# Mixer outputs read back early, HGRN2 keys scaled on VectorE, decay products beside the transposes

## The chip, the cores and the metric

The kernel runs on one core of one Trainium2 chip. The metric is device time in microseconds (us); lower is better. Engines are named as the profile names them: PE is TensorE (matmuls; PEld its weight loads), DVE is VectorE, ACT is ScalarE, POOL is GpSimd, SP is SyncE. A row whose engine ends in q (SPq, ACTq) is that engine issuing a transfer.

## The reference, cut to what matters

One layer is computed for a prompt of 1024 tokens and for 8 samples of 4 tokens each, so 1056 columns in all (`T`), in fp32:

```python
h = _rmsnorm(x, g_attn)
z = h @ w_in      # one projection, 6152 columns: q/k/v/a/b/out-gate of branch A, q/f/i/out-gate of branch B, two gates
# branch A (gated DeltaNet): causal conv of width 4 on q/k/v, SiLU, then the chunked gated delta rule
# branch B (HGRN2): f = lb + (1-lb)*sigmoid(fb); attention with decay exp(cumsum(log f)), in chunks
y_a = (_head_rmsnorm(o_a) * silu(oga)) @ w_branch_a
y_b = (_head_rmsnorm(o_b) * silu(ogb)) @ w_branch_b
mix = jax.nn.sigmoid(gate_a) * y_a + jax.nn.sigmoid(gate_b) * y_b
x = x + mix @ w_out
h2 = _rmsnorm(x, g_ffn)
gc, new_ffn = _causal_conv(h2 @ w_ffn_gate, ffn_buf, w_ffn_conv)      # width 3
x = x + (jax.nn.silu(gc) * (h2 @ w_ffn_up)) @ w_ffn_down
```

Model width 1024, four heads of 128 in each branch, FFN width 2816. The new states and convolution caches are outputs too.

## The kernel before, in words

**Products.** Every large product is made of three matmuls on two halves of each operand. `split` casts fp32 to `hi` (ACT, L83) and subtracts to get `lo` (DVE, L84); `mm3` then adds hi·hi (L109), hi·lo (L110) and lo·hi (L111). A weight is loaded by `load_w` (SP, L96, tile `wraw`) and split into `whi` and `wlo`. The activations of the first projection are `hhi` and `hlo`; the same two memory slots later hold `ohi` and `olo`, the split outputs of the two branches.

**Stages.** The start loads and normalises x. Then come the two mixers: four groups of 256 tokens of HGRN2 (`hgrn_group`, about 160 to 460 us of the profiled execution), and four of gated DeltaNet (`gdn_group`, about 460 to 790 us). Mixers are chains of small steps on PE, DVE, ACT and POOL. To fill PE's time in between, the columns of the first projection are computed by and by: `fill` holds a queue of projections, and each mixer generator hands back a number at its `yield`, which says how many steps of 24 matmuls (352 columns wide, so 24 × 0.16 us) `drive` records there. What remains of the queue is computed after the last group (`fill.drain()`). Then follow the branch projections and the merge, `w_out`, and the FFN, which are matmul after matmul.

**Order.** The kernel is written in Tile: a scheduler decides the order of each engine's instructions from priorities in order of the code and from its own estimate of readiness. Each engine and each queue runs its rows strictly in that order. A tile whose pool slot was used before waits until the earlier tile's last reader is done; by default a pool that takes over memory of a closed pool waits for all of that pool.

**One HGRN2 group** (`hgrn_attn`) has seven levels. A level is: matmuls of `kk` with `qf` on PE (L997, or L984 for the last two levels), a masked copy of their result into `ad` (DVE, L1004), then `qf` times the running decay (DVE, L1010) and `kk` times the running decay (POOL, L1011). The next level's matmuls need both. `conv_proj` (the width-4 convolution of branch A's q, k, v, and the FFN's convolution) runs among them: its tile `z` gets a zero pad and the cached rows from POOL (L212, L213), the projected columns from ACT (L218), and three of its taps are DVE operations (L231, tile `co`).

**One gated DeltaNet group** transposes q, k, v on PE (L689), copies them, then for each chunk and head builds a decay matrix `EE` (DVE L709 makes `A`, PE L710 multiplies it, ACT L711 takes the exponential, and DVE masks it), and uses it on the k·q product (PE L718, DVE L719 into `UA`). A triangular inverse follows on DVE, through memory and back (`dU`, `dX`), and its first matmul is L773.

**From mixers to branch projections.** Each group's outputs `og` go to HBM (`oT_d`; ACT's queue, L874). After the mixers' pool is closed, `raw` is loaded back from `oT_d` by three transfers on SP's queue (2112, 1536 and 576 KB, L1172), behind a load of the sample rows `x1s` (L1165), and is split into `ohi` and `olo`, 16 casts and 16 subtractions. The last two of the three transfers are written with two fill steps ahead of each. In the branch projection `sga` and `sgb` are the gates, loaded from `sg_d` (L1195).

Of the kernel before, what the change touches and what calls it, by code (L numbers as in the profile page):

```python
# [8 lines left out]
F32 = mybir.dt.float32  # L9
# [33 lines left out]
def hybrid_step(ctx: ExitStack, tc: tile.TileContext, ins, outs):  # L43
# [28 lines left out]
    nc.gpsimd.memset(pexp[:, 1, :], 0.5)  # L72

# [131 lines left out]
    def conv_proj(W, j, width, wT, cacheT, out_cache, dst, dst_s, zp, src=None):  # L205

        pad = width - 1
        per = pad + STEP
        zw = pad + SEQ + NBAT * per
        z = zp.tile([P, zw], F32, name="z", tag="z")  # L210
        zs = z[:, pad + SEQ:].rearrange("p (b t) -> p b t", t=per)
        nc.gpsimd.memset(z[:, 0:pad], 0.0)  # L212
        nc.gpsimd.tensor_copy(zs[:, :, 0:pad], cacheT.rearrange("p (b t) -> p b t", t=pad))  # L213

        def ev(nb, ps):
            a = nb * BW
# [42 lines left out]
    def qkv_work(W, j, kind, h, zp=None):  # L259
# [3 lines left out]
                             qkv_s[:, kind, h, :], zp or mp)  # L263
# [9 lines left out]
    def load_x(t):  # L273
        xts[t] = n1.tile([P, D], F32, name="xt", bufs=6)
        nc.sync.dma_start(out=xts[t][:rows(t)], in_=x_rows(t))
# [198 lines left out]
    def decay_beta():  # L474
        nc.scalar.activation(beta, ab[:, :, 4:8], AF.Sigmoid)
        uy = mp.tile([P, 4, NT, H], F32, name="uy", tag="z")
# [39 lines left out]
    qf_s = mp.tile([P, 2, H, 32], F32, name="qf_s", bufs=1)  # L516
    og_s = mp.tile([P, 2, H, 32], F32, name="og_s", bufs=1)

    junk = mp.tile([P, P], BF16, name="junk", bufs=1)

    def os_tile(shape, name):
        return mp.tile(shape, F32, name=name, tag="os", bufs=4)
# [84 lines left out]
    def sample_products(src, cols, nk):  # L607
# [7 lines left out]
        ps = [PSM() for _ in range(nk)]  # L615
# [52 lines left out]
    def gdn_group(g, St):  # L668
# [16 lines left out]
        sst = mp.tile([P, 2, 8], F32, name="sst")  # L685
        for p in range(8):
            ps = PSM()
# [4 lines left out]
            nc.scalar.activation(junk, ps[:, 2 * P:3 * P], AF.Square, accum_out=sst[:, 1, p:p + 1])  # L692
            yield 0.1
# [8 lines left out]
        nc.vector.tensor_tensor(pr, pr, beta[:, c0:c0 + 2, :].rearrange("p c h -> p (c h)"), ALU.mult)  # L702
        for p0 in range(0, 8, 4):
            EE = os_tile([P, 4, P], "EE")
            ps = PSM()
            for p in range(p0, p0 + 4):
                cc, h = pairs[p]
                A = mp.tile([P, P], F32, name="A")
                nc.vector.tensor_scalar(A, slow, gcol[:, c0 + cc, h:h + 1], None, op0=ALU.mult)  # L709
                nc.tensor.matmul(ps[:, (p - p0) * P:(p - p0 + 1) * P], A, tri, start=True, stop=True)  # L710
            nc.scalar.activation(EE.rearrange("p c i -> p (c i)"), ps, AF.Exp)  # L711
            nc.vector.tensor_tensor(EE, EE, eem[:, 1:2, :].broadcast_to([P, 4, P]), ALU.mult)
# [8 lines left out]
            yield 0.5  # L721
# [105 lines left out]
        o_sb = os_tile([P, 8, P], "o_sb")  # L827
# [43 lines left out]
        og = mp.tile([P, H, GW], F32, name="og", tag="z")  # L871
# [84 lines left out]
    def hgrn_attn(q, f, kk, tots, nch, nlev, attn, ad):  # L956
# [15 lines left out]
        for l in range(nlev):  # L972
# [38 lines left out]
            nc.gpsimd.tensor_tensor(kv[:, :, 0, :], kv[:, :, 0, :], tv[:, :, 1:2].broadcast_to(shp), ALU.mult)  # L1011
# [4 lines left out]
            yield 0.75  # L1016
        return tot

    def hgrn_group(g, St, attn, ad):
# [18 lines left out]
        o_sb = os_tile([P, 8, P], "o_sb")  # L1038
# [23 lines left out]
        og = mp.tile([P, H, GW], F32, name="og", tag="z")  # L1062
# [93 lines left out]
    store_conv_cache(cout, 12, 27, cq_p[0, 0], cq_s.rearrange("l b t c -> (l b t) c"), mp, "z")  # L1156
# [16 lines left out]
    fill.drain()  # L1173
    ohi = hslot(0, [P, 2 * H, T], F32R, "ohi")
# [214 lines left out]
```

## Time and profile before

| | |
|---|---|
| time, median of 3 runs | 1808.07 us (1807.83 to 1810.8) |
| the profiled execution | 1809.22 us, its span 1807.5 us |
| PE busy | 1730.7 us, 96% of the span |
| PEld busy | 1637.3 us, 91% |
| DVE busy | 877.2 us, 49% |
| ACT busy | 529.1 us, 29% |
| POOL busy | 183.0 us, 10% |
| moved by DMA | 159.52 MB, 88 GB/s over the span |

The profiled execution is 1.7 us longer than its span, and stands 1.15 us above the median, inside the runs. PE is the engine that is nearly always busy; the others work beside it. So the time is PE's busy time and its idle time, and each idle stretch of PE has a row that names what ended it.

### The profile page before, as it was taken

Reading aid. Unit: us, or ns where it says so; the run is one execution under the profiler, and the core shown is the slowest. Engines: PE = TensorE matmul, PEld = TensorE weight load, DVE = VectorE, ACT = ScalarE, POOL = GpSimd, SP = SyncE. Lnnn points to the kernel's source line nnn. Section 1 sums busy time; section 2 is a strip of 40 time slices with the busy share of each in tenths; the row PEclk is TensorE's granted clock in tenths of the full one; section 3 lists DMA queues with packets and bytes.
Section 4 is the critical chain, followed back from the end, with each engine's and each line's share of the span. In section 5 each row is a group of like instructions: output and inputs, shape, how many; then the busy total and the mean of one; then the engine's idle time right before and its main releaser. Section 6 shows DMA issues by size and latency. Waiting matters only on the chain.

```text
span 1807.5 us, 31280 instructions
## 1 busy us (share of the span) xinstructions
PE 1730.7 (96%) x13277; PEld 1637.3 (91%) x13277; DVE 877.2 (49%) x1478; ACT 529.1 (29%) x1158; POOL 183.0 (10%) x323
## 2 busy tenths in 40 slices
PE   7999899989999989987999999999999999999997
PEld 7999899889889988987999999989989899899896
DVE  5411545785535364435542734453453453554457
ACT  5443323433433343332110522112112112122122
POOL 2200213341101020100000100000000000000001
PEclk9999999999999899998999999999999999999999
DMA  7333234345254243236432211111111111111103
GB/s 210 96 101 110 90 111 141 118 129 159 75 161 116 92 141 106 61 104 200 138 104 87 59 48 36 52 40 41 44 47 47 47 47 47 47 48 47 47 27 109
DMA packets 200648, 159.52 MB, mean 88 GB/s; under 512 B 18638, under 2 KB 185184, under 8 KB 200489
## 3 DMA queue, kind: packets, MB, share of 16 engines
q1 hardware_dynamic: 171286, 119.14, 22.3%
q10 hardware_dynamic: 29222, 38.39, 6.2%
q8 instruction: 104, 1.70, 0.4%
q14 instruction: 36, 0.29, 0.1%
HBM read 117.74 MB, written 39.69 MB: 87 GB/s over the span
## 4 chain that ended last, share of the span: by engine, by line
PE 55%; DVE 4%; DMA 2%; ACT 1%; issue 1%; POOL 1%; SPq 0%; ACTq 0%; DVEq 0%; POOLq 0%
PE pd L109 17%; PE pd L110 17%; PE pd L111 17%; PE pd L121 1%; DVE y L1348 1%; DMA raw<-oT_d 1%; DVE Pt L752 0%; DVE tmp L177 0%; PE pd L120 0%; ACT tmp L174 0%; DVE X L754 0%; POOL rs L76 0%; DVE mlo L84 0%; PE pd L123 0%; DMA Yd<-dX 0%
## 5 line engine op out<-in xcount | busy, mean ns | idle before, releaser
L109 PE MATMUL pd<-hhi,whi 128*128 128x352 f32 x1056 | 350.7, 332 | 0.0
L111 PE MATMUL pd<-hhi,wlo 128*128 128x352 f32 x1056 | 345.7, 327 | 0.0
L110 PE MATMUL pd<-hlo,whi 128*128 128x352 f32 x1056 | 344.6, 326 | 0.0
L109 PE MATMUL pd<-mhi,whi 128*128 128x352 f32 x1056 | 340.5, 323 | 0.0
L110 PE MATMUL pd<-mlo,whi 128*128 128x352 f32 x1056 | 338.6, 321 | 0.6 <-DVE mlo L84 0.6
L111 PE MATMUL pd<-mhi,wlo 128*128 128x352 f32 x1056 | 338.3, 321 | 0.0
L84 DVE TENSOR_TENSOR wlo<-wraw,whi 128x1024 fp32r<-128x1024 f32 x126 | 155.4, 1242 | 213.4 <-ACT whi L83 213.0
L83 ACT CAST whi<-wraw 128x1024 fp32r<-128x1024 f32 x126 | 130.4, 1049 | 399.4 <-PE pd L111 202.0
L109 PEld LDWEIGHTS pd<-hhi,whi 128*128 128x128 f32 x1056 | 200.3, 190 | 2.0 <-issue 0.6
L110 PEld LDWEIGHTS pd<-hlo,whi 128*128 128x128 f32 x1056 | 200.6, 190 | 0.8
L111 PEld LDWEIGHTS pd<-hhi,wlo 128*128 128x128 f32 x1056 | 200.4, 190 | 0.8
L110 PEld LDWEIGHTS pd<-mlo,whi 128*128 128x128 f32 x1056 | 198.4, 188 | 1.3 <-DVE mlo L84 0.9
L109 PEld LDWEIGHTS pd<-mhi,whi 128*128 128x128 f32 x1056 | 198.0, 188 | 0.4
L111 PEld LDWEIGHTS pd<-mhi,wlo 128*128 128x128 f32 x1056 | 198.0, 188 | 0.0
L1315 DVE TENSOR_TENSOR x<-x,pd 128x512 f32<-128x512 f32 x176 | 119.0, 686 | 78.0 <-PE pd L111 77.7
L109 PE MATMUL pd<-whi,act 128*128 128x512 f32 x352 | 138.1, 392 | 0.1
L110 PE MATMUL pd<-wlo,act 128*128 128x512 f32 x352 | 137.2, 390 | 0.0
L111 PE MATMUL pd<-whi,act 128*128 128x512 f32 x352 | 137.0, 389 | 0.0
L218 ACT COPY z<-pd 128x352 f32<-128x352 f32 (+1 forms) x102 | 44.1, 442 | 141.6 <-PE pd L111 138.3
L1292 DVE TENSOR_TENSOR ga<-pd,ga 128x352 f32<-128x352 f32 x66 | 34.5, 523 | 98.5 <-PE pd L111 98.5
L109 PEld LDWEIGHTS pd<-whi,act 128*128 128x128 f32 x352 | 66.1, 188 | 16.2 <-PE pd L111 1.6
L109 PE MATMUL pd<-ohi,whi 128*128 128x352 f32 x192 | 62.8, 328 | 18.3 <-ACT ohi L83 18.3
(418 smaller groups left out, 2622.8 us busy)
## 6 DMA issues: line engine op xcount, KB each, us to landing
wraw<-in_w_in SPq DMA_DIRECT2D x48, 512.0 KB, 4.5
wraw<-in_w_ffn_gate SPq DMA_DIRECT2D x22, 512.0 KB, 4.4
wraw<-in_w_ffn_up SPq DMA_DIRECT2D x22, 512.0 KB, 3.8
wraw<-in_w_ffn_down SPq DMA_DIRECT2D x22, 512.0 KB, 4.4
sg_d<-sg ACTq DMA_DIRECT2D x16, 528.0 KB
qkv_d<-sl ACTq DMA_DIRECT2D x12, 512.0 KB, 3.6
sga<-sg_d SPq DMA_DIRECT2D x12, 352.0 KB, 7.0
sgb<-sg_d SPq DMA_DIRECT2D x12, 352.0 KB, 2.9
```

Of the source, the lines that this page charges most:

```text
L83: nc.scalar.copy(out=hi, in_=src)
L84: (eng or nc.vector).tensor_tensor(lo, src, hi.bitcast(F32), ALU.subtract)
L109: nc.tensor.matmul(ps, whi[:, kw], xhi[:, kx], start=q == 0, stop=False)
L110: nc.tensor.matmul(ps, whi[:, kw], xlo[:, kx], start=False, stop=False)
L111: nc.tensor.matmul(ps, wlo[:, kw], xhi[:, kx], start=False, stop=q == n - 1)
L121: nc.tensor.matmul(ps[:NS], st[:, kx, 0:NS], wlo[:, kw], start=False, stop=False)
L218: nc.scalar.copy(out=z[:, pad + a:pad + e], in_=ps[:, :e - a])
L1292: nc.vector.tensor_tensor(a[:, bs], ps, a[:, bs], ALU.mult)
L1315: nc.vector.tensor_tensor(x1[:, t, qs], x1[:, t, qs], ps, ALU.add)
L1348: nc.vector.scalar_tensor_tensor(yt[:n, qs], x1t(t)[:n, qs], rs[:n], last["g"][:n, qs], ALU.mult, ALU.mult)
```

## The change

Five things are changed, in the code's order.

1. `conv_proj`: the zero pad and the cached rows of `z` are copied by ACT (from a constant tile `zero`), no longer by POOL.
2. Pools: the mixers' tiles `z`, `uy`, `og` and three small ones move into a pool of their own (`mz`); `o_sb` gets a tile of its own, and the tag `os` has three buffers in place of four; `xt` has five in place of six. The sample products of each branch go into one PSUM bank, cleared by one matmul with `zero`, in place of one or two banks.
3. `gdn_group`: the decay matrices `EE` (the operations of L709 to L712) are made inside the loop of the transposes; the yields around them are 0.2 (new) and 0.4 (was 0.5).
4. `hgrn_attn`: `kk` is scaled on DVE, no longer on POOL; the yield of a level is 0.7 (was 0.75).
5. The boundary: the pool `post` waits tile by tile (`reuse_waits="tile"`), `raw` is its first tile, and the load of `x1s` comes behind the loads of `raw`.

```diff
+    zero = const.tile([P, P], F32, name="zero")
+    nc.gpsimd.memset(zero, 0.0)
+
...
-        nc.gpsimd.memset(z[:, 0:pad], 0.0)
-        nc.gpsimd.tensor_copy(zs[:, :, 0:pad], cacheT.rearrange("p (b t) -> p b t", t=pad))
+        nc.scalar.copy(out=z[:, 0:pad], in_=zero[:, 0:pad])
+        nc.scalar.copy(out=zs[:, :, 0:pad], in_=cacheT.rearrange("p (b t) -> p b t", t=pad))
...
     def os_tile(shape, name):
-        return mp.tile(shape, F32, name=name, tag="os", bufs=4)
+        return mp.tile(shape, F32, name=name, tag="os", bufs=3)
...
-        ps = [PSM() for _ in range(nk)]
+        ps = PSM()
+        nc.tensor.matmul(ps[:, :nk * P], zero, cols.rearrange("p a h t -> p (a h t)"), start=True, stop=False,
+                         skip_group_check=True)
...
-                    nc.tensor.matmul(ps[a][32 * h:32 * h + 32, 0:P], zc[:, a * H + h, 32 * b:32 * b + 32],
-                                     Sb[:, h, :], start=b == 0, stop=b == NBAT - 1, skip_group_check=True)
...
+        EEs = []
         for p in range(8):
+            cc, h = pairs[p]
             ps = PSM()
             for q, kind in enumerate((0, 2, 1)):
                 nc.tensor.transpose(out=ps[:, q * P:(q + 1) * P], in_=col(kind, p), identity=ident)
             nc.vector.tensor_copy(kvt[:, p].rearrange("p a d -> p (a d)"), ps[:, 0:2 * P])
             nc.scalar.activation(junk, ps[:, 0:P], AF.Square, accum_out=sst[:, 0, p:p + 1])
             nc.scalar.activation(junk, ps[:, 2 * P:3 * P], AF.Square, accum_out=sst[:, 1, p:p + 1])
+            if p % 4 == 0:
+                pe = PSM()
+            A = mp.tile([P, P], F32, name="A")
+            nc.vector.tensor_scalar(A, slow, gcol[:, c0 + cc, h:h + 1], None, op0=ALU.mult)
+            nc.tensor.matmul(pe[:, (p % 4) * P:(p % 4 + 1) * P], A, tri, start=True, stop=True)
+            if p % 4 == 3:
+                EE = os_tile([P, 4, P], "EE")
+                nc.scalar.activation(EE.rearrange("p c i -> p (c i)"), pe, AF.Exp)
+                nc.vector.tensor_tensor(EE, EE, eem[:, 1:2, :].broadcast_to([P, 4, P]), ALU.mult)
+                EEs.append(EE)
             yield 0.1
         pr = mp.tile([P, 8], F32, name="pr")
...
+        yield 0.2
         for p0 in range(0, 8, 4):
-            EE = os_tile([P, 4, P], "EE")
-            ps = PSM()
-            for p in range(p0, p0 + 4):
-                cc, h = pairs[p]
-                A = mp.tile([P, P], F32, name="A")
-                nc.vector.tensor_scalar(A, slow, gcol[:, c0 + cc, h:h + 1], None, op0=ALU.mult)
-                nc.tensor.matmul(ps[:, (p - p0) * P:(p - p0 + 1) * P], A, tri, start=True, stop=True)
-            nc.scalar.activation(EE.rearrange("p c i -> p (c i)"), ps, AF.Exp)
-            nc.vector.tensor_tensor(EE, EE, eem[:, 1:2, :].broadcast_to([P, 4, P]), ALU.mult)
+            EE = EEs[p0 // 4]
             nc.vector.tensor_tensor(kgs[:, p0:p0 + 4], EE[:, :, P - 1], pr[:, p0:p0 + 4], ALU.mult)
             for p in range(p0, p0 + 4):
...
-            yield 0.5
+            yield 0.4
...
-        o_sb = os_tile([P, 8, P], "o_sb")
+        o_sb = mp.tile([P, 8, P], F32, name="o_sb", bufs=1)
...
             nc.vector.tensor_tensor(qv[:, :, 1, :], qv[:, :, 1, :], tv[:, :, 0:1].broadcast_to(shp), ALU.mult)
-            nc.gpsimd.tensor_tensor(kv[:, :, 0, :], kv[:, :, 0, :], tv[:, :, 1:2].broadcast_to(shp), ALU.mult)
...
-            yield 0.75
+            yield 0.7
         return tot
...
-    store_conv_cache(cout, 12, 27, cq_p[0, 0], cq_s.rearrange("l b t c -> (l b t) c"), mp, "z")
+    store_conv_cache(cout, 12, 27, cq_p[0, 0], cq_s.rearrange("l b t c -> (l b t) c"), mz, "z")
     for gen in side:
         drive(gen)
...
-    post = ctx.enter_context(tc.tile_pool(name="post", bufs=1))
+    post = ctx.enter_context(tc.tile_pool(name="post", bufs=1, reuse_waits="tile"))
+    raw = post.tile([P, 2 * H, T], F32, name="raw", tag="m1")
     mhi = post.tile([P, KD, T], F32R, name="mhi", tag="m0")
     x1s = post.tile([32, D], F32, name="x1s")
-    nc.sync.dma_start(out=x1s, in_=x_rows(NC))
-    raw = post.tile([P, 2 * H, T], F32, name="raw", tag="m1")
     last = (NG - 1) * GW
     for x, a, b in ((1, 0, T), (0, 0, last), (0, last, T)):
         if a:
@@ -1171,6 +1181,7 @@
             fill.step()
         nc.sync.dma_start(out=raw[:, x * H:(x + 1) * H, a:b], in_=oT_d[x][:, :, a:b].rearrange("h p t -> p h t"))
     fill.drain()
+    nc.sync.dma_start(out=x1s, in_=x_rows(NC))
     ohi = hslot(0, [P, 2 * H, T], F32R, "ohi")
```

**SP's queue at the boundary** (names: `raw` is the read-back, `wraw` the next weights of the branch projection, `sga` and `sgb` the gates, `res` rows of x for `w_out`). Before:

```order
L1195 DMA sga<-sg_d_92 128x2x352
L96 DMA wraw<-in_w_branch_a 128x4x128
L96 DMA wraw<-in_w_branch_b 128x4x128
L1165 DMA x1s<-in_x_sample 32x1024
L1172 DMA raw<-oT_d_91 128x4x1056
L1172 DMA raw<-oT_d_90 128x4x768
L1172 DMA raw<-oT_d_90 128x4x288
L1195 DMA sgb<-sg_d_93 128x2x352
```

With the change:

```order
L1206 DMA sga<-sg_d_94 128x2x352
L1182 DMA raw<-oT_d_93 128x4x1056
L1182 DMA raw<-oT_d_92 128x4x768
L1182 DMA raw<-oT_d_92 128x4x288
L1184 DMA x1s<-in_x_sample 32x1024
L1206 DMA sgb<-sg_d_95 128x2x352
L1206 DMA sga<-sg_d_94 128x2x352
L1239 DMA res<-in_x_prompt 128x2x256 x3
L99 DMA wraw<-in_w_branch_a 128x4x128
L99 DMA wraw<-in_w_branch_b 128x4x128
```

The three loads of `raw` have moved ahead of a pair of weight loads and of `x1s`, directly behind the first `sga`.

**ACT at the same place** (`sg` is the last gate that the fill computes; `whi` a cast of branch weights). Before:

```order
L564 ACTIVATE sg<-pd 128x352
L83 CAST whi<-wraw 128x8x128
L565 DMA sg_d_93<-sg 128x1056
L83 CAST ohi<-raw 128x352 x4
L83 CAST ohi<-raw 128x2x352 x4
L83 CAST ohi<-raw 128x352 x4
L83 CAST ohi<-raw 128x2x352 x4
```

With the change:

```order
L568 ACTIVATE sg<-pd 128x352
L86 CAST ohi<-raw 128x352
L569 DMA sg_d_95<-sg 128x1056
L86 CAST ohi<-raw 128x352 x7
L86 CAST ohi<-raw 128x2x352 x8
L86 CAST whi<-wraw 128x8x128 x2
```

The first four and the next four rows of before are branch B's part of `raw`; branch A's, with which the first product begins, came after them. Now the eight narrow casts, of both branches' first 352 columns, stand first, and two weight casts stand behind all sixteen.

**DVE in the second HGRN2 group** (`ad` is the masked copy of a level's result, `qf` and `kk` the scaled operands, `co` the convolution, `wlo` a weight's low half). Before:

```order
L1004 COPY_PREDICATED ad<-lmask_u,pm 128x64x2
L1010 TENSOR_TENSOR qf<-qf,tots 128x256x2
L1004 COPY_PREDICATED ad<-lmask_u,pm 128x32x4
L1010 TENSOR_TENSOR qf<-qf,tots 128x128x4
L84 TENSOR_TENSOR wlo<-wraw,whi 128x8x128
L229 TENSOR_SCALAR co<-z,cwT 128x1080
L1004 COPY_PREDICATED ad<-lmask_u,pm 128x16x8
L231 SCALAR_TENSOR_TENSOR co<-z,cwT,co 128x1080
L1010 TENSOR_TENSOR qf<-qf,tots 128x64x8
```

With the change:

```order
L1015 COPY_PREDICATED ad<-lmask_u,pm 128x64x2
L1021 TENSOR_TENSOR qf<-qf,tots 128x256x2
L1022 TENSOR_TENSOR kk<-kk,tots 128x256x2
L1015 COPY_PREDICATED ad<-lmask_u,pm 128x32x4
L1021 TENSOR_TENSOR qf<-qf,tots 128x128x4
L1022 TENSOR_TENSOR kk<-kk,tots 128x128x4
L87 TENSOR_TENSOR wlo<-wraw,whi 128x8x128
L232 TENSOR_SCALAR co<-z,cwT 128x1080
L1015 COPY_PREDICATED ad<-lmask_u,pm 128x16x8
L234 SCALAR_TENSOR_TENSOR co<-z,cwT,co 128x1080
L1021 TENSOR_TENSOR qf<-qf,tots 128x64x8
L234 SCALAR_TENSOR_TENSOR co<-z,cwT,co 128x1080
```

Each level's scaling of `kk` now stands on DVE behind that of `qf`, and at the last level shown a convolution tap stands between the two.

## Rows read from the trace of the kernel before

**Rows 1.** Stretches of the span: length, busy PE, PEld, DVE, ACT, POOL, clock, DMA.

```profile
160.00:460.00 300.00, 278.80 (x3404) 265.42 (x3403) 172.15 (x241) 106.01 (x276) 74.66 (x90) 0.99 0.41 125
460.00:790.00 330.00, 315.07 (x2886) 293.13 (x2887) 163.81 (x427) 128.26 (x363) 45.67 (x61) 0.97 0.35 106
...
800.00:820.00 20.00, 7.36 (x50) 6.98 (x49) 2.45 (x2) 4.41 (x7) 0.00 (x0) 0.74 0.64 216
820.00:840.00 20.00, 13.97 (x73) 13.52 (x74) 14.31 (x23) 9.41 (x17) 0.00 (x0) 0.74 0.65 214
...
sum 1807.50, PE 1730.73 PEld 1637.32 DVE 877.18 ACT 529.14 POOL 183.00; mean PE 157.34 PEld 148.85 DVE 79.74 ACT 48.10 POOL 16.64
```

**Rows 2.** PE's timeline at the boundary: start, length, [idle before <-releaser].

```profile
807.04 0.32 PE L111 MATMUL pd<-hhi,wlo 128*128 128x352 f32 x1
825.65 0.96 PE L109 MATMUL pd<-ohi,whi 128*128 128x352 f32 x2 [18.29 <-ACT ohi L83]
826.99 0.66 PE L110 MATMUL pd<-olo,whi 128*128 128x352 f32 x1 [0.39 <-DVE olo L84]
```

**Rows 3.** The chain of waits, 805 to 832 us: start, length, what.

```profile
809.57 0.37 SPq L96
...
811.56 9.12 DMA raw<-oT_d
820.85 4.76 ACT ohi L83 x9
825.62 1.33 DVE olo L84 x2
...
829.71 0.29 PE pd L109
...
830.82 0.16 PE pd L109
```

**Rows 4.** Timeline of SP's queue, 786 to 835 us, the last issue before 809.57.

```profile
797.28 0.37 SPq L1195 DMA_DIRECT2D sga<-sg_d  x1
```

**Rows 5.** Timelines of ACT, its issues included, 796 to 832 us.

```profile
799.42 0.38 ACTq L874 DMA_DIRECT2D oT_d<-og  x1
...
820.85 8.63 ACT L83 CAST ohi<-raw 128x352 fp32r<-128x352 f32 x16 [11.27 <-DMA raw<-oT_d]
```

**Rows 6.** Timeline of DVE, 818 to 832 us.

```profile
821.37 10.09 DVE L84 TENSOR_TENSOR olo<-raw,ohi 128x352 fp32r<-128x352 f32 x16 [10.53 <-ACT ohi L83]
```

**Rows 7.** PE's groups, 160 to 460 us: busy, mean ns | idle before, releasers.

```profile
L997 PE MATMUL pm<-qf,kk 128*32 128x16 f32 x1280 | 15.1, 186 | 13.1 <-DVE qf L1010 6.6 <-POOL kk L1011 2.5 <-DVE qf L969 2.0
...
L984 PE MATMUL pm<-qf,kk 128*32 128x32 f32 (+1 forms) x192 | 7.3, 206 | 3.3 <-DVE qf L1010 1.9 <-POOL kk L1011 1.4
```

**Rows 8.** Timeline of all engines in one HGRN2 level, 188.3 to 190.9 us.

```profile
188.54 0.45 DVE L1004 COPY_PREDICATED ad<-lmask_u,pm 128x128 f32<-128x128 uint8 x1 [0.63 <-PE pm L997]
188.64 1.31 POOL L1011 TENSOR_TENSOR kk<-kk,tots 128x512 f32<-128x512 f32 x1 [1.58 <-PE pm L997]
...
188.79 1.71 DVE L1010 TENSOR_TENSOR qf<-qf,tots 128x512 f32<-128x512 f32 x1
...
190.64 0.43 PE L997 MATMUL pm<-qf,kk 128*32 128x16 f32 x31 [0.84 <-DVE qf L1010]
```

**Rows 9.** Instructions of L1010, L1011, L231: ns min/median/max, first and last start.

```profile
L1010 DVE TENSOR_TENSOR qf<-qf,tots x24: 677/736/1710, 188.8 to 401.8; 128x512 f32<-128x512 f32 x24
...
L1011 POOL TENSOR_TENSOR kk<-kk,tots x24: 1079/1283/2051, 188.6 to 401.9; 128x512 f32<-128x512 f32 x24
...
L231 DVE SCALAR_TENSOR_TENSOR co<-z,cwT,co x36: 1317/1342/2386, 253.7 to 445.3; 128x1080 f32<-128x1080 f32 x36
```

**Rows 10.** PE's groups, 460 to 800 us, columns as in the seventh group.

```profile
L710 PE MATMUL pm<-eem,A 128*128 128x128 f32 x64 | 11.1, 295 | 1.4 <-DVE A L709 1.4
...
L773 PE MATMUL pm<-Xd,UA 32*32 32x16 f32 x256 | 2.9, 180 | 2.4 <-DVE Xd L767 2.4
```

More of the change, by code (lines that the diff above doesn't have):

```diff
@@ L262, in qkv_work @@
         yield from conv_proj(W, j, 4, cwT[:, ti, 24:28], cwT[:, ti, 0:24], cout[:, ti, :], t[:, :SEQ],
-                             qkv_s[:, kind, h, :], zp or mp)
+                             qkv_s[:, kind, h, :], zp or mz)
         nc.scalar.dma_start(out=qkv_d[kind, h], in_=t[:, :SEQ])
@@ L273, in load_x @@
     def load_x(t):
-        xts[t] = n1.tile([P, D], F32, name="xt", bufs=6)
+        xts[t] = n1.tile([P, D], F32, name="xt", bufs=5)
         nc.sync.dma_start(out=xts[t][:rows(t)], in_=x_rows(t))
@@ L475, in decay_beta @@
         nc.scalar.activation(beta, ab[:, :, 4:8], AF.Sigmoid)
-        uy = mp.tile([P, 4, NT, H], F32, name="uy", tag="z")
+        uy = mz.tile([P, 4, NT, H], F32, name="uy", tag="z")
         u, y, w, a = (uy[:, k] for k in range(4))
@@ L515, in hybrid_step @@
     mp = mixp.enter_context(tc.tile_pool(name="mix", bufs=2))
-    qf_s = mp.tile([P, 2, H, 32], F32, name="qf_s", bufs=1)
-    og_s = mp.tile([P, 2, H, 32], F32, name="og_s", bufs=1)
-    junk = mp.tile([P, P], BF16, name="junk", bufs=1)
+    mz = mixp.enter_context(tc.tile_pool(name="mixz", bufs=2))
+    qf_s = mz.tile([P, 2, H, 32], F32, name="qf_s", bufs=1)
+    og_s = mz.tile([P, 2, H, 32], F32, name="og_s", bufs=1)
+    junk = mz.tile([P, P], BF16, name="junk", bufs=1)
     def os_tile(shape, name):
-        return mp.tile(shape, F32, name=name, tag="os", bufs=4)
+        return mp.tile(shape, F32, name=name, tag="os", bufs=3)
     def bc(ap, n):
@@ L627, in sample_products @@
                 for h in range(H):
-                    nc.tensor.matmul(ps[a][32 * h:32 * h + 32, 0:P], zc[:, a * H + h, 32 * b:32 * b + 32],
-                                     Sb[:, h, :], start=b == 0, stop=b == NBAT - 1, skip_group_check=True)
+                    nc.tensor.matmul(ps[32 * h:32 * h + 32, a * P:(a + 1) * P], zc[:, a * H + h, 32 * b:32 * b + 32],
+                                     Sb[:, h, :], start=False, stop=b == NBAT - 1, skip_group_check=True)
             yield 0.2
-        return [p[:, 0:P] for p in ps]
+        return [ps[:, a * P:(a + 1) * P] for a in range(nk)]
     def sample_update(src, dst, keys, u, scale):
@@ L870, in gdn_group @@
         need(*[("og", 0, h) for h in range(H)])
-        og = mp.tile([P, H, GW], F32, name="og", tag="z")
+        og = mz.tile([P, H, GW], F32, name="og", tag="z")
         nc.sync.dma_start(out=og, in_=og_d[0][:, :, gs].rearrange("h p t -> p h t"))
@@ L1010, in hgrn_attn @@
             nc.vector.tensor_tensor(qv[:, :, 1, :], qv[:, :, 1, :], tv[:, :, 0:1].broadcast_to(shp), ALU.mult)
-            nc.gpsimd.tensor_tensor(kv[:, :, 0, :], kv[:, :, 0, :], tv[:, :, 1:2].broadcast_to(shp), ALU.mult)
+            nc.vector.tensor_tensor(kv[:, :, 0, :], kv[:, :, 0, :], tv[:, :, 1:2].broadcast_to(shp), ALU.mult)
             nt = tots[:, off:off + nblk // 2]
@@ L1037, in hgrn_group @@
         yield 0.3
-        o_sb = os_tile([P, 8, P], "o_sb")
+        o_sb = mp.tile([P, 8, P], F32, name="o_sb", bufs=1)
         oss = mp.tile([P, 8], F32, name="pss")
@@ L1061, in hgrn_group @@
         need(*[("og", 1, h) for h in range(H)])
-        og = mp.tile([P, H, GW], F32, name="og", tag="z")
+        og = mz.tile([P, H, GW], F32, name="og", tag="z")
         nc.sync.dma_start(out=og, in_=og_d[1][:, :, gs].rearrange("h p t -> p h t"))
```

## The prediction

> **What bounds the kernel now.** First the stretches of the span: PE is busy 1730.7 of 1807.5 us, so only 76.8 us can be won without taking work away, and the question is where they lie. The two HGRN2/DeltaNet stretches hold 300 − 278.8 = 21.2 us and 330 − 315.1 = 14.9 us of it; the 40 us around the boundary hold 40 − 7.36 − 13.97 = 18.7 us, at a granted clock of 0.74 [rows 1]. The rest lies at the two ends, which the change leaves as they are.
>
> Next PE's timeline at the boundary, which shows that those 18.7 us are one gap. The last fill matmul ends at 807.36; the first of the branch projections begins at 825.65, and the row says that it waited 18.29 us for ACT's cast of `ohi`, then 0.39 us for DVE's `olo` [rows 2]. The chain of waits says what ACT itself waited for: a weight cast and its subtraction end at 809.57, only then SP issues the weights behind them, then `x1s`, and at 811.56 `raw`, which takes 9.12 us; five of the sixteen casts and two subtractions that PE does not need first make up most of the remaining 5 us [rows 3]. SP had issued a gate load at 797.28 and then nothing for 12 us [rows 4]: the loads of `raw` stood behind a weight load whose buffer came free late. The data itself was ready earlier: the last `og` was sent off at 799.42 [rows 5].
>
> Last the mixers, by PE's groups: in HGRN2 the levels' matmuls L997 and L984 waited 13.1 + 3.3 us, mostly for `qf` (L1010) and `kk` (L1011) [rows 7]; in DeltaNet no line waited over 5 us, L773 2.4 and L710 1.4 [rows 10].
>
> **The boundary.** In the new order `raw` stands directly behind the gate load, so it can go at 797.28 + 0.37 = 797.65 [rows 4] if its tile is free; its memory's last readers are of the last DeltaNet group, whose output leaves at 799.42 [rows 5]. Only the third, 576 KB transfer needs that output. PE's first product needs the first two, 2112 + 1536 = 3648 KB. What they take is not shown alone, so two bounds: if the 9.12 us [rows 3] were for the 2112 KB only, 15.8 us, landing at 813.4; if they were for all that was issued together, 9.1 us, landing at 806.8, before the fill ends. The DMA engines were busy 0.64 and 0.65 of the two stretches at the boundary, with weights and gates among the traffic [rows 1], so I take a landing near 809.
>
> Then the splits set the start, for `ohi` takes the slot of `hhi`, free only when the fill's last matmul has read it. Sixteen casts took 8.63 us, so a cast of the mean width 0.54 [rows 5], a subtraction 0.63 [rows 6]; narrow ones are shorter. The first product begins with branch A's first cast, the fifth: 5 × 0.54 = 2.7 us after the fill, and 3.0 with the hand-over; its second matmul needs the fifth subtraction, 0.54 + 5 × 0.63 + 0.3 = 4.0 us after it. Later casts keep ahead: PE spends 48 matmuls, 7.7 us, on each third of the columns, whose eight casts take 4.3. With half a microsecond for a PSUM bank that frees late (DVE stands in the subtractions), the gap is 4.5 us; with the late landing 813.4 + 0.54 + 0.63 − 807.36 = 7.2 us. Gain: 18.29 + 0.39 − 4.5 = **14.2 us**, range 11.5 to 15.2.
>
> The first matmuls after the gap ran at half clock, 0.29 us apart at 829.71 and 0.16 at 830.82 [rows 3]; from 826.99 that is 3.6 us, of which 1.6 were lost. I expect the short gap to leave this as it is; it is a gain of 1.6 at most. The weight casts that now stand behind the sixteen casts end some 11 us after the fill; they are for the next pair of columns, needed 144 matmuls × 0.16 = 23 us after PE's start, so they are covered. If the fill's end moves, with the 116 matmuls that now stand behind the last group (111 before, counted in the orders), PE has them to do anyway.
>
> **HGRN2.** In the level shown, the masked copy starts at 188.54, `qf` runs 188.79 to 190.50, and PE starts at 190.64: 2.10 us [rows 8]. POOL's `kk` ran 188.64 to 189.95, and `qf` took 1.71 us where its median is 0.736 and its shortest 0.677 for the same shape [rows 8, 9]. So the long `qf` is `kk`'s neighbour's price, and on DVE alone the level is 0.25 + 2 × 0.70 + 0.14 = 1.79 us. By that the move gains only 0.3 us where the two start together; where POOL came alone at 1.283 [rows 9], nothing. The larger part comes from the fill: counted in PE's order, the first group's levels stood 6 or 7 fill matmuls apart (1.1 us) and now 9 to 11 (1.6). Some 12 levels then wait about 0.3 us each, 3.6 us; the wait for L969, 2.0 [rows 7], I leave; and taps of the convolution, 1.342 us each [rows 9], now stand between `qf` and `kk` at a few levels, three of which I count, 4.0. That leaves 9.6 of 16.4: a gain of **7 us**. Bounds: 13 if the cover hides everything but such a tap or two, 0 if a tap is exposed at all 12 short levels (12 × 1.34 = 16 us).
>
> Here a rule of the Trainium skill bears on the trace. In the rows POOL started first and DVE's operation ended 0.55 us after POOL's [rows 8]. SBUF — State Buffer, section "Who interferes with whom", says that a VectorE instruction with two SBUF inputs and a GpSimd instruction that reads SBUF share a port, and that the first holds it for its whole length; by that `qf` would have ended 0.70 after POOL, and goes back to 0.70 once POOL is gone. The trace agrees but for 0.15 us. If instead `qf` kept its 1.71, the level would take 2.8 us, and the 12 short levels would wait 1.2 rather than 0.3: 11 us lost, and the total some 1799.
>
> **DeltaNet.** The exponentials and masks now stand earlier, so L710's 1.4 us can go [rows 10]. Against it stand the fill's counts: from a group's last L718 to L773 stood 161, 163, 161 and 157 fill matmuls, now 150, 151, 162 and 159. If the inverse takes as long as before, L773 waits 11 × 0.16 and 12 × 0.16 us more in the first two groups, less 0.5 in the others: +3.2. Net between −1.4 and +3.2; I take **+1**.
>
> **The rest.** The zero matmul comes twice, with 256 columns at most; L710 takes 0.295 us for 128 [rows 10], so 0.6 each at most, +0.5 for both as most lies in waits. ACT's 68 small pad copies are none longer than a cast of `ohi`, 0.54; in the mixers 24 of them are 13 us at most on an engine busy 106 of 300 and 128 of 330 us [rows 1], behind the activation that frees the tile. If ACT were the bound there, those 13 us would show; POOL's waits for that tile hurt nobody but `kk`. Fewer `os` and `xt` buffers: none holds a tile that the next one waits for.
>
> **Sum.** −14.2 − 7 + 1 + 0.5 = −19.7 against the profiled 1809.22: 1789.5. That execution stood 1.15 us over the median, so **1788 us**; the case's own range is 1783 to 1793.
>
> **Rivals.**
> - *Better (0.12).* The fill covers every level, −13 in place of −7, and the clock's losses shrink. At 0.97 of 330 us and 0.99 of 300 [rows 1] the half clock cost 13 us in the mixers; shorter waits could bring back half. 1788 − 6 − 6 = 1776.
> - *Mixers give nothing (0.18).* HGRN2 at its bound of 0 for the taps: 1788 + 7 = 1795; with L773 at +3.2, 1797.
> - *`raw` is still late (0.10): the change doesn't do what it says.* Something on SP or in the old pool holds it until about 806; then it lands at 815 to 822, the gap is 9 to 16 us, the boundary gains 3 to 10: 1792 to 1799. For it speaks that three kinds of waits meet on that tile; against it that SP stood idle from 797.65 [rows 4].
> - *Slower (0.06).* DVE becomes the bound in HGRN2: 28 `kk` operations of 0.70 join 36 taps of 1.342 between 253.7 and 445.3 [rows 9]. Each level that finds one more tap in its chain costs 1.34; from 15 such levels the 20 us won are gone, and with all 21 levels of the three groups that meet convolutions (28 us) the time is 1816. Against it: DVE was busy 172 of 300 us [rows 1], and most levels there stand 24 or more fill matmuls apart, 3.8 us.
> - *Cancelled within 0.2% (0.02 by itself).*
>
> The forecast has 0.52. Cases up to 1800 and down from 1776 hold over 0.8, so the range is **1775 to 1801**. A difference under 0.2% (3.6 us) can't be told from none: faster 0.90, same 0.04, slower 0.06.
>
> **What would show it.** Right: `raw` issued near 798; PE's gap at the boundary 4 to 5 us, ended by `olo` or `ohi`; the 40 us around it with some 32 us of PE; `kk` and `qf` at 0.70 each; L997 and L984 waiting under 10 us; L773 some 5. Wrong: `raw` issued after 800, a gap ended by the transfer, levels that wait for taps, or half-clock stretches longer than before.

## The result and the profile after

The changed kernel takes 1784.6 us, median of 4 runs (1782.43 to 1785.84), against 1809.08 for the kernel before in the same runs: ratio 0.9863, 95% interval 0.9846 to 0.988. The profiled execution is 1784.54 us, its span 1782.4. PE is busy 1731.6 us, 0.9 more than before, so the 25.1 us of span are idle time of PE that has gone: between 160 and 840 us, summed over windows of 10 us, it fell from 54.8 to 28.5, by 26.3.

The windows of the changed kernel, columns as in [rows 1] (length, busy time of PE, PEld, DVE, ACT and POOL, clock, DMA); the first two answer to the first two rows there, the other two to the boundary's:

```profile
160.00:460.00 300.00, 290.07 (x3483) 273.94 (x3482) 182.44 (x311) 118.42 (x330) 35.41 (x42) 1.00 0.41 127
460.00:780.00 320.00, 310.41 (x2844) 291.55 (x2844) 148.88 (x390) 111.34 (x329) 40.50 (x59) 0.95 0.36 107
...
780.00:800.00 20.00, 12.49 (x85) 12.14 (x83) 1.66 (x3) 3.61 (x8) 0.00 (x0) 0.87 0.83 300
800.00:820.00 20.00, 18.53 (x106) 18.33 (x107) 18.06 (x29) 10.70 (x18) 0.00 (x0) 0.87 0.62 188
```

The HGRN2 stretch is idle for 9.9 us where it was 21.2; the boundary's 40 us hold 31.0 us of PE, 9.7 more than before. The granted clock rose from 0.99 to 1.00 in HGRN2 and fell from 0.97 to 0.95 in DeltaNet. PE's timeline at the boundary answers to [rows 2]:

```profile
792.16 0.32 PE L114 MATMUL pd<-hhi,wlo 128*128 128x352 f32 x1
801.47 0.96 PE L112 MATMUL pd<-ohi,whi 128*128 128x352 f32 x2 [8.98 <-ACT ohi L86]
```

The gap is 8.98 us where it was 18.29 + 0.39. SP's queue there, answering to [rows 4]:

```profile
782.16 0.37 SPq L1206 DMA_DIRECT2D sga<-sg_d  x1
782.70 13.91 SPq L1182 DMA_DIRECT2D raw<-oT_d  x3
796.76 0.39 SPq L1184 DMA_DIRECT2D x1s<-in_x_sample  x1
```

The read-back goes out behind the gate load, 9.8 us ahead of the fill's end, and its third part only at the end of that row's 13.91 us, when the last output is written. ACT's timeline says what the gap now waits for:

```profile
785.24 0.38 ACTq L885 DMA_DIRECT2D oT_d<-og  x1
...
796.31 0.57 ACT L250 COPY rowt<-pm 27x512 f32<-27x512 f32 x1 [11.72 <-DMA oT_d<-og]
796.79 0.45 ACT L568 ACTIVATE sg<-pd 128x352 f32<-128x352 f32 x1
...
798.88 0.46 ACT L568 ACTIVATE sg<-pd 128x352 f32<-128x352 f32 x1 [0.68 <-DMA out<-rowt]
799.24 0.48 ACT L86 CAST ohi<-raw 128x352 fp32r<-128x352 f32 x1
```

The 512 KB write of the last output was issued 2.5 us after 3.6 MB of reads and took 11 us to land; of the four such writes in the HGRN2 stretch of the kernel before, the profile has a landing time of 3.6 us (last column, us from issue to landing):

```profile
oT_d<-og ACTq DMA_DIRECT2D x4, 512.0 KB, 3.6
```

A copy of the convolution's cache rows (`rowt`) takes that output's slot, so it waited 11.72 us for the write, at the head of ACT's queue; two gate evacuations, another `rowt` and all casts of `ohi` stood behind it, 6.7 us beyond the fill's end at 792.5. The second part of `raw` landed late as well, by the same columns:

```profile
raw<-oT_d SPq DMA_DIRECT2D x1, 1536.0 KB, 14.0
```

Issued at 783.1, it landed at about 797, 4.6 us beyond the fill's end but 2 us ahead of ACT's first cast, so in this kernel nothing waits for it.

PE's groups between 160 and 450 us (busy, mean ns | idle before, releasers) answer to [rows 7]:

```profile
L1008 PE MATMUL pm<-qf,kk 128*32 128x16 f32 x1280 | 15.0, 185 | 2.0 <-DVE kk L1022 1.3 <-DVE qf L980 0.6
...
L995 PE MATMUL pm<-qf,kk 128*32 128x32 f32 (+1 forms) x192 | 7.4, 206 | 0.5 <-DVE kk L1022 0.5
```

The instructions of the two scalings, ns min/median/max, answer to [rows 9]; first `qf`:

```profile
L1021 DVE TENSOR_TENSOR qf<-qf,tots x24: 673/691/1531, 187.2 to 381.3; 128x512 f32<-128x512 f32 x24
```

and `kk`, now on DVE:

```profile
L1022 DVE TENSOR_TENSOR kk<-kk,tots x24: 669/684/686, 187.8 to 383.1; 128x512 f32<-128x512 f32 x24
```

The level matmuls wait 2.5 us in place of 16.4. The longest wait that is left has a convolution tap in its chain; DVE's timeline there, and PE's row:

```profile
358.76 0.68 DVE L1021 TENSOR_TENSOR qf<-qf 128x512 f32<-128x512 f32 x1
359.36 1.33 DVE L234 SCALAR_TENSOR_TENSOR co<-z,cwT,co 128x1080 f32<-128x1080 f32 x1
360.62 0.68 DVE L1022 TENSOR_TENSOR kk<-kk,qf 128x512 f32<-128x512 f32 x1
```

```profile
361.44 0.72 PE L1008 MATMUL pm<-qf,kk 128*32 128x16 f32 x64 [0.99 <-DVE kk L1022]
```

In DeltaNet, PE's groups between 450 and 790 us have the inverse's first matmul, which waited 2.4 [rows 10]:

```profile
L784 PE MATMUL pm<-Xd,UA 32*32 32x16 f32 x256 | 2.9, 180 | 5.0 <-DVE Xd L778 5.0
```

Against it a line that is not among [rows 7] and [rows 10] has lost its wait, the product of `um` with the cached states `st`. PE's groups over both stretches, before and then with the change:

```profile
L656 PE MATMUL pm<-um,st 96*128 96x512 f32 x16 | 7.2, 453 | 4.6 <-DVE UA L719 2.3 <-DVE um L653 1.6 <-ACT junk L692 0.7
```

```profile
L662 PE MATMUL pm<-um,st 96*128 96x512 f32 x16 | 7.2, 447 | 0.4 <-DVE um L659 0.4
```

### The profile page after: what moved, and what is told of

It is laid out like the page before. It is cut to its first block, busy times and chain, and to the rows that moved or that the text cites. A ratio compares the mean times of both kernels' runs of the same rounds, so it can differ in the third digit from the quotient of the medians.

```text
span 1782.4 us, 31161 instructions
## 1 busy us (share of the span) xinstructions
PE 1731.6 (97%) x13281; PEld 1638.0 (92%) x13281; DVE 870.2 (49%) x1508; ACT 524.5 (29%) x1220; POOL 136.4 (8%) x226
## 4 chain that ended last, share of the span: by engine, by line
PE 82%; DVE 8%; DMA 5%; issue 2%; ACT 2%; POOL 2%; SPq 0%; ACTq 0%; DVEq 0%; POOLq 0%
PE pd L112 24%; PE pd L114 24%; PE pd L113 24%; DVE co L234 1%; DMA oT_d<-og 1%; DVE Pt L763 1%; PE pd L124 1%; DVE X L765 1%; PE pm L1008 1%; DVE y L1359 1%; DMA qf<-qf_d 1%; PE pd L123 1%; DMA Sb<-in_state_delta 1%; PE pm L1054 0%; PE pm L865 0%
## 5 line engine op out<-in xcount | busy, mean ns | idle before, releaser
L112 PEld LDWEIGHTS pd<-whi,act 128*128 128x128 f32 x352 | 66.0, 188 | 16.1 <-PE pd L114 1.8
L114 PEld LDWEIGHTS pd<-whi,act 128*128 128x128 f32 x352 | 66.1, 188 | 14.1
```

The costliest lines, as they stand in the source:

```text
L112: nc.tensor.matmul(ps, whi[:, kw], xhi[:, kx], start=q == 0, stop=False)
L114: nc.tensor.matmul(ps, wlo[:, kw], xhi[:, kx], start=False, stop=q == n - 1)
```

## The experiments

Twelve kernels ran, four to a chip, each four beside the kernel before on the same chip; so between chips ratios are compared, not times. The kernel before had medians of 1807.18, 1809.34 and 1806.76 us on the three.

**The boundary's own edits undone.** Changed kernel with

```diff
-    post = ctx.enter_context(tc.tile_pool(name="post", bufs=1, reuse_waits="tile"))
-    raw = post.tile([P, 2 * H, T], F32, name="raw", tag="m1")
+    post = ctx.enter_context(tc.tile_pool(name="post", bufs=1))
     mhi = post.tile([P, KD, T], F32R, name="mhi", tag="m0")
     x1s = post.tile([32, D], F32, name="x1s")
+    nc.sync.dma_start(out=x1s, in_=x_rows(NC))
+    raw = post.tile([P, 2 * H, T], F32, name="raw", tag="m1")
...
     fill.drain()
-    nc.sync.dma_start(out=x1s, in_=x_rows(NC))
```

> The changed kernel with its boundary as before (the pool waits for all of the old pool; the sample rows are loaded ahead of the read-back; the read-back tile is not the first of its pool), all else kept. Theory: the early read-back is worth the shrinking of the boundary gap from 18.3 to 9.0 us. Undone, the loads go out only when the last cache rows are out, near 798 to 800, the gap is 15 to 18 us, and the time 1791 to 1794. Rival: what counts is that no weight load stands ahead of the read-back any more, which stays so here; then the gap grows by 3 us at most and the time is 1785 to 1788.

1783.89 us (1775.62 to 1786.03), ratio 0.9864 (0.984 to 0.9888): the rival, with a time just under its 1785. Its SP queue:

```profile
781.29 0.35 SPq L1176 DMA_DIRECT2D x1s<-in_x_sample  x1
781.68 13.07 SPq L1183 DMA_DIRECT2D raw<-oT_d  x3
```

and PE's timeline:

```profile
801.65 1.25 PE L112 MATMUL pd<-ohi,whi 128*128 128x352 f32 x3 [11.48 <-ACT ohi L86]
```

The read-back goes out 8.5 us ahead of the fill's end, near the 9.8 with them. The gap is 2.5 us longer, as the rival had it (3 at most); the runs spread over 10 us, so the time does not show it. So of the five edits the fifth is not what brings `raw` forward.

**The boundary's edits alone**, the same lines on the kernel before.

> The kernel before with the boundary edits alone. In its order of SP the read-back still stands behind the third pair of branch weights, whose buffer comes free at 809.6. Theory (the queue decides): the gap stays 16 to 18.5 us and the time 1806 to 1809. Rival (waiting tile by tile is enough): the gap falls to 9 us or less and the time to 1799.

1805.78 us, ratio 0.9991 (0.9974 to 1.0009): no difference. In its SP queue the weight loads stand ahead of `raw` still:

```profile
803.89 0.37 SPq L96 DMA_DIRECT2D wraw<-in_w_branch_a  x1
804.32 0.57 SPq L96 DMA_DIRECT2D wraw<-in_w_branch_b  x1
805.18 1.82 SPq L1171 DMA_DIRECT2D raw<-oT_d  x3
```

and PE's timeline has the old gap, near enough:

```profile
819.21 0.95 PE L109 MATMUL pd<-ohi,whi 128*128 128x352 f32 x2 [17.52 <-ACT ohi L83]
```

**The second mixers' pool alone**, on the kernel before:

```diff
+    mz = mixp.enter_context(tc.tile_pool(name="mixz", bufs=2))
-    qf_s = mp.tile([P, 2, H, 32], F32, name="qf_s", bufs=1)
+    qf_s = mz.tile([P, 2, H, 32], F32, name="qf_s", bufs=1)
...
-        og = mp.tile([P, H, GW], F32, name="og", tag="z")
+        og = mz.tile([P, H, GW], F32, name="og", tag="z")
...
-    store_conv_cache(cout, 12, 27, cq_p[0, 0], cq_s.rearrange("l b t c -> (l b t) c"), mp, "z")
+    store_conv_cache(cout, 12, 27, cq_p[0, 0], cq_s.rearrange("l b t c -> (l b t) c"), mz, "z")
```

and the same for `og_s`, `junk`, `uy` and the tiles of `conv_proj`.

> The kernel before with the second mixers' pool alone (z, uy, og and the small tiles in a pool of their own; boundary, keys and decay matrices as before). Its order of SP has the read-back ahead of the third weight pair. Theory: it is this split of the pool that lets the read-back go early, since the memory that it takes is then free when the last group's products are done; the boundary gap falls from 18.3 to 9 to 12 us and the time to 1798 to 1802. Rival (the split needs the tile-wise waits or the smaller tags): 1805 to 1809.

1799.89 us, ratio 0.9952 (0.9937 to 0.9966): as the theory had it. SP's queue:

```profile
793.13 0.35 SPq L1166 DMA_DIRECT2D x1s<-in_x_sample  x1
793.53 14.12 SPq L1173 DMA_DIRECT2D raw<-oT_d  x3
```

PE's timeline:

```profile
813.17 0.95 PE L109 MATMUL pd<-ohi,whi 128*128 128x352 f32 x2 [11.07 <-ACT ohi L83]
```

So the split alone brings `raw` ahead of the third weight pair. The likely reason is that the memory which `post` takes over no longer holds the cache rows and the last output, which are in use longest; no run shows this reason by itself.

**What is left of the gap.** Three kernels on the changed one. First, the cache rows stored before the first DeltaNet group: the call of `store_conv_cache` stands ahead of `side.append(gdn_sample())`.

> The changed kernel with the convolution-cache rows transposed and stored before the first DeltaNet group, not after the last. Theory: what is left of the gap (9.0 us) comes from ACT, whose copy of the cache rows waits 11.7 us for the last group's output to be written, since it takes that tile's slot, and the casts of the read-back stand behind it. Without that the casts start at the fill's end, the gap is 4 to 6 us and the time 1779 to 1782. Rival: the read-back itself lands only near 799, beside the output's write, and the gap stays 8 to 9 us: 1784 to 1785.

1788.76 us, ratio 0.9915 (0.9886 to 0.9944): slower than the changed kernel, so neither expectation holds. The gap did shrink, to 7.33 us, and its end is another one. SP's queue:

```profile
802.39 13.70 SPq L1182 DMA_DIRECT2D raw<-oT_d  x3
```

ACT's timeline:

```profile
812.29 0.48 ACT L86 CAST ohi<-raw 128x352 fp32r<-128x352 f32 x1
812.72 2.62 ACT L86 CAST ohi<-raw 128x352 fp32r<-128x352 f32 x5
817.76 5.72 ACT L86 CAST ohi<-raw 128x352 fp32r<-128x352 f32 x10 [2.42 <-DMA raw<-oT_d]
```

Here the landing sets the gap: the second part of `raw` came 15.4 us after the first issue, and ACT waited 2.42 us for it. The profiled execution shows a loss in the DeltaNet groups, which the early rows reordered: PE was busy 286.4 of the 305 us from 455 to 760, at a clock of 0.94, where the changed kernel has 295.0 at 0.95. But that execution took 1802.05 us, the longest of the six and 13 over their median, so how much of the median's loss lies there is not shown.

Second, all cache rows in one tile, which takes the free slot:

```diff
-    store_conv_cache(cout, 12, 27, cq_p[0, 0], cq_s.rearrange("l b t c -> (l b t) c"), mz, "z")
+    def store_qkv_cache(src, dst_p, dst_s):
+        rt = mz.tile([64, 8 * P], F32, name="rowt", tag="z")
+        for i, k0 in enumerate((0, 4, 8)):
...
+            nc.scalar.copy(out=rt[b:b + 27, c:c + 512], in_=ps[:27])
...
+    store_qkv_cache(cout, cq_p[0, 0], cq_s.rearrange("l b t c -> (l b t) c"))
```

> The changed kernel with all cache rows in one tile, which takes the free slot and not that of the last output. Theory (ACT is held by the wait for the output's write): the casts start within 1.5 us of the fill's end, and the gap is 5 us: 1780 to 1781. Rival (the transfer bounds as well: in the run with early rows the read-back's second part took 15.4 us from its issue): the gap is 6.5 to 8 us and the time 1782 to 1784.

Third, the read-back with the first 352 columns of both branches first:

```diff
-    for x, a, b in ((1, 0, T), (0, 0, last), (0, last, T)):
-        if a:
+    for x, a, b in ((1, 0, BW), (0, 0, BW), (1, BW, T), (0, BW, last), (0, last, T)):
+        if x == 0 and a:
```

> The changed kernel with the read-back cut so that both branches' first 352 columns are loaded first (1.4 MB ahead of the rest). Theory (ACT is held by the wait for the output's write): no change, gap 9 us, 1783 to 1786. Rival (the landing of the first product's data sets the gap): gap 5 us, 1780 to 1781.

And both:

> Both of the last two edits on the changed kernel. If either wait alone would set the gap, only both together close it: gap 3.5 to 5 us, 1779 to 1781. If one of the two single edits already has that, this one adds nothing.

They took 1778.93, 1778.78 and 1779.36 us: ratios 0.9828 (0.9806 to 0.985), 0.984 (0.9816 to 0.9863) and 0.9843 (0.9823 to 0.9864), with gaps of 5.76, 6.67 and 5.35 us. All are quicker in the median than the changed kernel (0.9863 itself), but all three intervals overlap with that kernel's, the first one's least, so by time the gain is unclear; what is shown is the gap. ACT's timeline in the first:

```profile
778.65 0.38 ACTq L885 DMA_DIRECT2D oT_d<-og  x1
...
787.74 0.47 ACT L86 CAST ohi<-raw 128x352 fp32r<-128x352 f32 x1
790.13 0.36 ACTq L569 DMA_DIRECT2D sg_d<-sg  x1
790.53 1.73 ACT L86 CAST ohi<-raw 128x352 fp32r<-128x352 f32 x4 [2.32 <-DMA oT_d<-og]
```

The first cast starts 1.2 us after the fill's end (786.55), as the theory had it; then an issue on ACT's queue (L569) stood in the way until 790.1, and the profile again names the output's write, 11.5 us after it was sent. In the second, ACT is held to the same point as in the changed kernel, yet the gap is 2.3 us shorter: PE starts half a microsecond after the first cast, not after the fifth, so the scheduler now casts what the first product needs first. Both expectations, no change and a gap of 5 us, missed that. ACT's timeline, and then PE's:

```profile
795.64 0.57 ACT L250 COPY rowt<-pm 27x512 f32<-27x512 f32 x1 [11.11 <-DMA oT_d<-og]
```

```profile
799.10 0.96 PE L112 MATMUL pd<-ohi,whi 128*128 128x352 f32 x2 [6.67 <-ACT ohi L86]
```

That both edits together gave no more than the first alone is the second branch of that expectation. In all three the profile names the output's write, sent beside the big reads, as what held ACT: the third kernel's last `rowt` transfer went out at 796.89, 11.0 us after the write. Writing the output ahead of the reads was not run.

**The keys back on GpSimd**, in the changed kernel:

```diff
-            nc.vector.tensor_tensor(kv[:, :, 0, :], kv[:, :, 0, :], tv[:, :, 1:2].broadcast_to(shp), ALU.mult)
+            nc.gpsimd.tensor_tensor(kv[:, :, 0, :], kv[:, :, 0, :], tv[:, :, 1:2].broadcast_to(shp), ALU.mult)
```

> The changed kernel with the keys scaled on GpSimd again, the yields kept. Theory: VectorE alone is quicker than the two engines beside each other (level 1.8 against 2.1 us), and GpSimd is late where it has other work; the waits of the level matmuls come back from 2.5 to 10 to 16 us, and the time is 1792 to 1798. Rival: the fill's new distance between levels hides the levels, whoever scales the keys: the waits stay under 6 us and the time is 1785 to 1788.

1795.36 us, ratio 0.9944 (0.9925 to 0.9964): the theory. By the ratios it is 0.8% slower than the changed kernel, some 15 us. PE's groups between 160 and 455 us:

```profile
L1008 PE MATMUL pm<-qf,kk 128*32 128x16 f32 x1280 | 14.8, 185 | 11.7 <-DVE qf L1021 11.5
L995 PE MATMUL pm<-qf,kk 128*32 128x32 f32 (+1 forms) x192 | 7.3, 206 | 2.5 <-POOL kk L1022 1.6 <-DVE qf L1021 0.7 <-DVE ad_s L1015 0.2
```

and DVE's timeline in one level:

```profile
188.90 0.45 DVE L1015 COPY_PREDICATED ad<-lmask_u,pm 128x128 f32<-128x128 uint8 x1 [0.63 <-PE pm L1008]
189.14 1.71 DVE L1021 TENSOR_TENSOR qf<-qf,tots 128x512 f32<-128x512 f32 x1
```

with PE's start behind it:

```profile
191.00 0.69 PE L1008 MATMUL pm<-qf,kk 128*32 128x16 f32 x62 [0.84 <-DVE qf L1021]
```

The long `qf` is back with GpSimd's `kk` (1.31 us from 189.00) beside it, and so is the fill's spacing: counted in PE's order, 6 or 7 matmuls between the first group's levels, at the same yields that gave 10 or 11 with the keys on DVE. So the spacing is the doing of the keys' engine, not of the yield. It looks as if the scheduler expects DVE to need longer for both and so puts more fill in between; its estimates were not looked at.

**The keys alone**, the line the other way on the kernel before, yield 0.75.

> The kernel before with the keys scaled on VectorE alone, the yield of a level 0.75 as before. Counted in its order of PE, the first group's levels stand 10 to 11 fill matmuls apart (before 6 to 7). Theory: the level matmuls' waits fall from 16 us to under 5 without the other edits: 1795 to 1799. Rival: the gain needs the changed yield or the pads off GpSimd: 1801 to 1806.

1792.62 us, ratio 0.9924 (0.9908 to 0.9939), better than the 1795 expected. L984 waited for nothing, and L997 5.4 us by PE's groups:

```profile
L997 PE MATMUL pm<-qf,kk 128*32 128x16 f32 x1280 | 15.1, 186 | 5.4 <-DVE kk L1011 4.2 <-DVE qf L969 1.1
```

**The pool and the keys together** on the kernel before.

> The kernel before with two of the edits, the second mixers' pool and the keys on VectorE. Theory: these two carry the whole change, and their gains add: 1784 to 1789. Rival: pads, decay matrices, tags and tile-wise waits carry a part: 1790 or more.

1780.92 us, ratio 0.9855 (0.9841 to 0.987): the whole change's 0.9863 (0.9846 to 0.988). It lies below the expected 1784, though the ratios of the two single runs would add to 0.9876, within the noise of this one. As the whole stands, the other edits together give nothing that shows; the last run below says why.

**The decay matrices late again**, in the changed kernel:

```diff
-            EE = EEs[p0 // 4]
+            EE = os_tile([P, 4, P], "EE")
+            ps = PSM()
...
-            yield 0.4
+            yield 0.5
```

with the lines of L709 to L712 back in this loop and the yield of 0.2 taken out.

> The changed kernel with the decay matrices made after the transposes, as before. Theory: the exchange of L710's waits for longer ones at the inverse's first matmul is even: 1782 to 1787. Rival: the move costs or gives over 4 us: below 1780 or above 1789.

1784.61 us, ratio 0.9879 (0.9864 to 0.9894): even, by the expected time; the inverse's first matmul waits 2.2 us where it was 5.0, and the product of `um` with `st` (L662) 4.2 where it was 0.4.

**The pads on GpSimd again**, in the changed kernel:

```diff
-        nc.scalar.copy(out=z[:, 0:pad], in_=zero[:, 0:pad])
-        nc.scalar.copy(out=zs[:, :, 0:pad], in_=cacheT.rearrange("p (b t) -> p b t", t=pad))
+        nc.gpsimd.memset(z[:, 0:pad], 0.0)
+        nc.gpsimd.tensor_copy(zs[:, :, 0:pad], cacheT.rearrange("p (b t) -> p b t", t=pad))
```

> The changed kernel with the convolution's pad and cached rows set by GpSimd again. Theory: GpSimd has nothing else there now that the keys are gone, so nothing changes: 1783 to 1787. Rival: the copies on ACT were worth something by themselves, since a late pad holds the projection's evacuation: 1788 or more.

1774.31 us, ratio 0.9814 (0.9798 to 0.9831): quicker than the changed kernel by 0.5%, outside both intervals, which neither expectation allowed. It is the quickest of all these kernels. It also parts from the two edits alone, timed on the same chip: 1780.92 there (1779.67 to 1782.48), 1774.31 here (1770.03 to 1775.82). By this comparison the edits beside the pool, the keys and the pads do give some 0.4% together, and the pads take it back; which of them gives it is not shown. The granted clock does not explain either difference: on that chip it was 0.989 to 0.993 in these runs, 0.989 to 0.991 with the two edits alone, and 0.987 to 0.991 with the decay matrices late, where the pads are on ACT and the time is 10 us longer. The windows of 360 to 455 us, where the first DeltaNet group begins, in the changed kernel and in this one:

```profile
360.00:455.00 95.00, 88.32 (x835) 83.40 (x835) 62.06 (x103) 44.02 (x131) 10.56 (x15) 1.00 0.45 137
```

```profile
360.00:455.00 95.00, 92.11 (x862) 87.77 (x860) 65.40 (x115) 43.88 (x121) 22.69 (x27) 1.00 0.44 137
```

PE is idle 3.8 us less there. The changed kernel's PE rows of that place, which have only the third left here, at 0.56 us:

```profile
431.97 0.49 PE L705 MATMUL pm<-eem,A 128*128 128x128 f32 x2 [1.03 <-DVE A L704]
434.62 0.33 PE L697 MATMUL pm<-ident,x 128*128 128x128 f32 x1 [2.00 <-DVE og_s L603]
442.42 0.33 PE L697 MATMUL pm<-ident,vx 128*128 128x128 f32 x1 [1.26 <-DMA vx<-qkv_d]
```

None of them waits for a pad. The pads alter the order on every engine, SP's `qf` loads included; and in the two profiled executions less of the span at half clock is, by estimate, another 3.5 us: one less the granted clock, times the window, summed from 160 to 840 us in windows of 10 us, is 20.5 in the changed kernel and 17.0 here. Which of the moved rows does it stays open.

## Why the prediction was right, and where its sums were off

The time, 1784.6 us, is 3.4 below the 1788 forecast, the fall between the medians 24.5 where the sum had 19.7: the forecast case. The mechanisms were the right ones, but both large terms lie outside their own ranges, one short and one beyond, and that the time came out so near is in part luck.

**The boundary** was forecast at −14.2, range 11.5 to 15.2, and gave −9.7. The step that failed is "Then the splits set the start, for `ohi` takes the slot of `hhi`": it was worked from the cast's slot and the landing near 809, and neither looked at what stands ahead of the casts in ACT's queue. The order has the copies of `rowt` there, ahead of the rows of it that were shown. The mis-sized piece is the output's write, 11 us beside the reads, taken as no matter for the first two parts. The landing was mis-sized as well: the sum took 11.4 us from the first issue (797.65 to 809), and the second part took about 14.4, inside the late bound of 15.8. With that landing the sum's own formula for a late one gives a gap of about 5.8 us; so by this estimate some 1.3 us of the 4.5 missed are the landing's and 3.2 ACT's. The run with all cache rows in one tile came to 5.76, though there an issue on ACT's queue held the casts too. The half-clock loss behind the gap stayed, as forecast: matmuls 0.29 us apart to 804.9. In the gap before, the working counts five casts where the row has nine [rows 3]; the sum does not use that count.

**Why `raw` went early** was put down to the new order as a whole, without saying which edit does it; the runs say that it is the split of the mixers' pool, not the tile-wise waits.

**HGRN2** was forecast at −7, 13 at most, and gave −13.9 on L997 and L984, −15.1 with the transposes of `kk` (L1035). The mechanism and the level's length were right (1.82 us from the masked copy at 186.95 to the matmuls at 188.77, forecast 1.79). With `kk` off GpSimd, `qf` has a median of 0.691 us, and with it back, 1.175, and 1.71 at the level shown. So the rule that the prediction took from the Trainium skill (SBUF — State Buffer, section "Who interferes with whom") held as used there. What was mis-sized is the rest of the 9.6 us that I left standing: 0.3 us at each short level and three exposed taps. Ten or eleven fill matmuls with their hand-over just cover 1.82 us, and taps were waited for at two levels only, 0.99 us in the rows shown and 0.34 at 373.9, 1.3 in place of 4.0; 2.5 us remained in all. The rival "mixers give nothing" fell with that, and so did "slower": DVE stood at 182 of 300 us.

**DeltaNet**: the wait of L773, forecast to grow by 3.2 us, grew by 2.6, and L710 kept 1.0 of its 1.4; but what is left of the 26.3 us without the boundary's 9.7 and the levels' 15.1 is a gain of 1.5 us, where +1 and +0.5 were forecast. The sum left out the product of `um` with `st` (L656), whose wait fell from 4.6 to 0.4 and comes back to 4.2 with the decay matrices late. So their move exchanges waits of like size and is worth nothing that shows, as forecast, though by a gain that was not counted.

**Signs of being wrong.** Two that the prediction named did show, small: levels that wait for a tap, and half-clock stretches longer than before in DeltaNet, where the clock is 0.95. From 160 to 840 us one less the clock, summed as above, is 23.8 before and 20.5 after, so HGRN2 and the boundary outweigh it. Executions of one kernel differ by as much: those with the old boundary had 0.986 to 0.994.

**Costed at nothing and wrong**: the pads. Their length was bounded well (0.18 and 0.20 us each, forecast 0.54 at most), and none is waited for, yet with them on ACT the kernel is 0.5% slower. The error is to cost instructions alone where an edit makes the scheduler place the rows of all engines anew; which row costs it is not shown.

## What to carry to other kernels

Where a scheduler places rows by its own estimate, price a moved instruction by how far apart it then sets the rows that wait, and read that from the order. Here the spacing grew by some four matmuls of 0.16 us and the level shortened from 2.10 to 1.82 us, so by these numbers the spacing was worth more; no run changed the one without the other. When a transfer is brought forward, look at which small write it will run beside and at who waits for that write in an in-order queue; here 512 KB took 11 us, and taking ACT's copy off that wait shortened the gap by 3.2 us. And take edits back one by one: two made as much as the whole, and a third, costed at nothing, took back 0.5%.

## What had not been expected of the hardware

A 512 KB write issued just behind 3.6 MB of reads landed 11 us later in the changed kernel (2.5 us behind) and 11.4 us later in the run with one tile of cache rows (1.9 us behind), against 3.6 us in the HGRN2 stretch of the kernel before. The DMA engines were busy 0.83 of that stretch (780 to 800 us) at 300 GB/s, against 0.41 at 125 in the HGRN2 stretch.
